# Row-wise cosine similarity: wide operations, a finer last block and an early finish of the first half

## Chip, cores and metric

The kernel runs on one core of one Trainium2 chip. The metric is the time of one execution on the device, in microseconds (us); lower is better. A span is the time from the first to the last instruction in a profile; it is about 1.8 us shorter than the time.

## The reference

For two float32 arrays of 8192 x 8192, one cosine similarity for each row:

```python
x_norm = np.linalg.norm(x, axis=1, keepdims=True)
y_norm = np.linalg.norm(y, axis=1, keepdims=True)
return np.sum(x * y, axis=1) / (x_norm.squeeze() * y_norm.squeeze() + 1e-8)
```

Each row needs three sums: of x·y, of x² and of y². The inputs are 537 MB, and every byte is used once.

## The kernel before

The 8192 rows are 64 blocks of 128 rows, one row for each partition. A block is one tile of x and one of y, 4 MB each. VectorE (DVE) makes the sum of products, ScalarE (ACT) both sums of squares, in two halves of 4096 columns (`CH`). x has three buffers and y two.

```python
def compute_chunk(xt, yt, b, c0, c1, slot):
    w = c1 - c0
    nc.vector.tensor_tensor_reduce(out=prod[:, :w], in0=xt[:, c0:c1], in1=yt[:, c0:c1],
        scale=1.0, scalar=0.0, op0=ALU.mult, op1=ALU.add, accum_out=dps[slot][:, b : b + 1])
    nc.scalar.activation(out=sq[:, :w], in_=xt[:, c0:c1], func=AF.Square, accum_out=sxs[slot][:, b : b + 1])
    nc.scalar.activation(out=sq[:, :w], in_=yt[:, c0:c1], func=AF.Square, accum_out=sys_[slot][:, b : b + 1])

for b in range(nblk):
    # ... cut: the tiles
    if not last:
        if b > 0:
            nc.sync.dma_start(out=xt, in_=x_v[b])
            nc.sync.dma_start(out=yt, in_=y_v[b])
        compute_chunk(xt, yt, b, 0, CH, 0)
        compute_chunk(xt, yt, b, CH, D, 1)
    else:
        cuts = [0, CH, CH + CH // 2, D]
        # ... cut: x and y of each piece are loaded in turn
        for j in range(3):
            compute_chunk(xt, yt, b, cuts[j], cuts[j + 1], j)
```

At the end all 64 columns of sums are added, the root is taken on ACT, DVE makes reciprocal and product, eight 32x32 transposes turn the 128 x 64 result, and one transfer stores it.

## Time and profile before

| what | value | view |
|---|---|---|
| time | 1265.75 us, median of 4 | runs |
| span | 1263.9 us | page |
| load queue | 98.8% of the span of 16 engines | queue table |
| load rate from 60 to 1200 us | 432 GB/s, DMA share 1.00 | stage table |
| DVE, ACT busy | 45%, 75% | page |
| loads end | about 1249 us | stages of 1 us |

The first fence is from the page: busy time of each engine, then the DMA queues with packets, MB and share of time.

```profile
DVE 571.1 (45%) x275; ACT 952.0 (75%) x519; POOL 0.5 (0%) x8
...
q1 hardware_dynamic: 19088, 536.91, 98.8%
q14 instruction: 9, 0.07, 0.0%
```

The second is the stage table of before. Its columns are: stretch in us, its length, busy time of DVE, ACT and POOL with counts of instructions, the granted clock, DMA share, GB/s.

```profile
60.00:1200.00 1140.00, 522.55 (x235) 869.00 (x469) 0.00 (x0) 1.00 1.00 432
...
1245.00:1246.00 1.00, 0.72 (x1) 0.97 (x3) 0.00 (x0) 1.00 0.96 401
1246.00:1247.00 1.00, 1.00 (x1) 1.00 (x1) 0.00 (x0) 1.00 0.26 107
...
1248.00:1249.00 1.00, 0.00 (x0) 1.00 (x2) 0.00 (x0) 1.00 0.14 57
```

The loads run at full rate until 1246 us and trickle out by about 1249. The 15 us after them are the tail. Its timeline follows: start, duration, engine, operation, tile, and in brackets the idle time before it and what ended that.

```profile
1230.45 3.62 ACT L74 ACTIVATE sscr<-yt 128x4096 bf16<-128x4096 f32 x1 [4.50 <-DMA yt<-in_y_dram]
...
1240.32 4.43 DVE L58 CUSTOM_DVE_ANT_0 pscr<-xt,yt 128x4096 bf16<-128x4096 f32 x1 [0.89 <-DMA yt<-in_y_dram]
1241.68 3.62 ACT L68 ACTIVATE sscr<-xt 128x4096 bf16<-128x4096 f32 x1
...
1255.26 1.91 ACT L74 ACTIVATE sscr<-yt 128x2048 bf16<-128x2048 f32 x1
1255.32 0.23 DVE L106 TENSOR_TENSOR sxf<-sxa,sx 128x64 f32<-128x64 f32 x1 [1.86 <-ACT sscr L68]
1255.47 2.29 DVE L58 CUSTOM_DVE_ANT_0 pscr<-xt,yt 128x2048 bf16<-128x2048 f32 x1
...
1257.96 0.22 DVE L112 TENSOR_TENSOR nxny<-sxf,syf 128x64 f32<-128x64 f32 x1
...
1261.07 0.55 SPq L129 DMA_DIRECT2D out_dram<-resT  x1
```

The second-last block's y lands at 1230.4. ACT then works without a pause until 1257, and begins the last block's first square only at 1241.68, though its first y piece, which lands after its x, is there at 1240.3. DVE's last product does not wait for data: it waits behind an add, which waits for ACT.

### The profile page before, as it was taken

To read this page: it belongs to the slowest core of one execution; us is meant where nothing else is said; L and a number is where in the kernel's file an instruction comes from. 1 tells how busy PE (TensorE), PEld (TensorE's weight loads), DVE (VectorE), ACT (ScalarE), POOL (GpSimd) and SP (SyncE) were. 2 spreads that over 40 slices of the span, in tenths; PEclk is the share of its full clock that TensorE was granted. 3 is DMA by queue.
4 is the path that set the end of the run, shared out by engine and by line. 5 is a ranking of instruction groups with operands and counts; after the bars stand their busy time and mean duration, and the time that the engine had idled before them with its cause. 6 is when DMAs were issued, how large, how long until landed. Compare 5 with 4: busy or idle time off the path is not lost.

```text
span 1263.9 us, 1239 instructions
## 1 busy us (share of the span) xinstructions
DVE 571.1 (45%) x275; ACT 952.0 (75%) x519; POOL 0.5 (0%) x8
## 2 busy tenths in 40 slices
DVE  2354353453543534535435345354353453544536
ACT  4787787877877878778777787787777877868777
POOL 0000000000000000000000000000000000000000
DMA  9999999999999999999999999999999999999994
GB/s 398 438 433 431 432 432 432 431 432 433 431 432 432 431 431 431 431 432 431 431 431 431 431 431 431 431 431 433 431 432 431 431 431 431 431 431 431 432 429 189
DMA packets 19097, 536.99 MB, mean 425 GB/s; under 512 B 2128, under 2 KB 2192, under 8 KB 2192
## 3 DMA queue, kind: packets, MB, share of 16 engines
q1 hardware_dynamic: 19088, 536.91, 98.8%
q14 instruction: 9, 0.07, 0.0%
HBM read 536.87 MB, written 0.03 MB: 425 GB/s over the span
## 4 chain that ended last, share of the span: by engine, by line
DMA 70%; ACT 25%; issue 5%; DVE 0%; ACTq 0%; SPq 0%; DVEq 0%
DMA yt<-in_y_dram 70%; ACT sscr L74 15%; ACT sscr L68 9%; DVE pscr L58 0%; DVE resT L125 0%; DVE rsq L117 0%; ACTq L74 0%; SPq L39 0%; ACT den L114 0%; DVE res L119 0%; DVEq L155 0%; DVE nxny L112 0%; DVE syf L106 0%; DVE dpf L106 0%; DVE dp L58 0%
## 5 line engine op out<-in xcount | busy, mean ns | idle before, releaser
L58 DVE CUSTOM_DVE_ANT_0 pscr<-xt,yt 128x4096 bf16<-128x4096 f32 x129 | 566.6, 4392 | 682.3 <-DMA yt<-in_y_dram 680.1
L74 ACT ACTIVATE sscr<-yt 128x4096 bf16<-128x4096 f32 x129 | 463.2, 3590 | 289.8 <-DMA yt<-in_y_dram 287.7
L68 ACT ACTIVATE sscr<-xt 128x4096 bf16<-128x4096 f32 x129 | 463.2, 3590 | 15.0 <-DMA xt<-in_x_dram 11.0
L74 ACT ACTIVATION_READ_ACCUMULATOR sscr<-yt 128x1 f32 x129 | 24.1, 187 | 0.0
L68 ACT ACTIVATION_READ_ACCUMULATOR sscr<-xt 128x1 f32 x129 | 24.1, 187 | 0.0
L58 DVE DVE_READ_ACCUMULATOR2_ANT dp<- 128x1 f32 x129 | 10.6, 82 | 0.0
L105 DVE TENSOR_TENSOR sxa<-sx,sx 128x64 f32<-128x64 f32 x1 | 0.2, 225 | 3.6 <-ACT sscr L68 3.6
L54 ACT ACT_TABLE_LOAD x1 | 1.3, 1283 | 0.7 <-PEq L144 0.7
L125 DVE STREAM_TRANSPOSE resT<-res 32x32 f32<-32x32 f32 x8 | 1.6, 201 | 0.1
L106 DVE TENSOR_TENSOR sxf<-sxa,sx 128x64 f32<-128x64 f32 x1 | 0.2, 225 | 1.9 <-ACT sscr L68 1.9
L105 DVE TENSOR_TENSOR sya<-sy,sy 128x64 f32<-128x64 f32 x1 | 0.2, 227 | 1.7 <-ACT sscr L74 1.7
L114 ACT ACTIVATE den<-nxny 128x64 f32<-128x64 f32 x1 | 0.3, 256 | 0.9 <-DVE nxny L112 0.9
L117 DVE RECIPROCAL rsq<-den 128x64 f32<-128x64 f32 x1 | 0.6, 553 | 0.3 <-ACT den L114 0.3
L119 DVE TENSOR_TENSOR res<-dpf,rsq 128x64 f32<-128x64 f32 x1 | 0.2, 224 | 0.0
L105 DVE TENSOR_TENSOR dpa<-dp,dp 128x64 f32<-128x64 f32 x1 | 0.2, 220 | 0.0
L106 DVE TENSOR_TENSOR syf<-sya,sy 128x64 f32<-128x64 f32 x1 | 0.2, 220 | 0.0
L106 DVE TENSOR_TENSOR dpf<-dpa,dp 128x64 f32<-128x64 f32 x1 | 0.2, 219 | 0.0
L112 DVE TENSOR_TENSOR nxny<-sxf,syf 128x64 f32<-128x64 f32 x1 | 0.2, 218 | 0.0
L54 ACT ACTIVATE rs_warm<-rs_warm 128x1 f32<-128x1 f32 x1 | 0.2, 203 | 0.0
L45 POOL MEMSET dp<- 128x64 f32 x1 | 0.2, 152 | 0.3 <-POOLq L144 0.3
L46 POOL MEMSET sx<- 128x64 f32 x1 | 0.2, 152 | 0.0
L47 POOL MEMSET sy<- 128x64 f32 x1 | 0.2, 152 | 0.0
(5 smaller groups left out, 0.5 us busy)
## 6 DMA issues: line engine op xcount, KB each, us to landing
xt<-in_x_dram SPq DMA_DIRECT2D x63, 4096.0 KB, 36.9
yt<-in_y_dram SPq DMA_DIRECT2D x63, 4096.0 KB, 27.6
xt<-in_x_dram SPq DMA_DIRECT2D x1, 2048.0 KB, 32.1
yt<-in_y_dram SPq DMA_DIRECT2D x1, 2048.0 KB, 17.9
xt<-in_x_dram SPq DMA_DIRECT2D x2, 1024.0 KB, 22.0
yt<-in_y_dram SPq DMA_DIRECT2D x2, 1024.0 KB, 24.0
out_dram<-resT SPq DMA_DIRECT2D x1, 32.0 KB, 1.8
```

The lines of the kernel that those rows point to most:

```text
L45: nc.gpsimd.memset(dps[2], 0.0)
L46: nc.gpsimd.memset(sxs[2], 0.0)
L47: nc.gpsimd.memset(sys_[2], 0.0)
L54: nc.scalar.activation(out=rs_warm, in_=rs_warm, func=AF.Sqrt, bias=0.0)
L58: nc.vector.tensor_tensor_reduce(out=prod[:, :w], in0=xt[:, c0:c1], in1=yt[:, c0:c1], scale=1.0, scalar=0.0, op0=ALU.mult, op1=ALU.add, ac ...
L68: nc.scalar.activation(out=sq[:, :w], in_=xt[:, c0:c1], func=AF.Square, accum_out=sxs[slot][:, b : b + 1],)
L74: nc.scalar.activation(out=sq[:, :w], in_=yt[:, c0:c1], func=AF.Square, accum_out=sys_[slot][:, b : b + 1],)
L105: nc.vector.tensor_tensor(out=a, in0=parts[0], in1=parts[1], op=ALU.add)
L106: nc.vector.tensor_tensor(out=f, in0=a, in1=parts[2], op=ALU.add)
L114: nc.scalar.activation(out=den, in_=nxny, func=AF.Sqrt, bias=0.0)
L117: nc.vector.reciprocal(out=rsq, in_=den)
L125: nc.vector.transpose(out=resT[S * j : S * j + S, S * i : S * i + S], in_=res[S * i : S * i + S, S * j : S * j + S],)
```

## The change

Its intent: one operation of 8192 columns in place of two of 4096 in blocks 0 to 61; the loads of block 62 in halves; the last block in pieces of 4096, 2048, 1024 and 1024, one y square given from ACT to DVE; the first 32 results finished at block 33; the last block's small sums on the idle POOL engine. The core of the diff:

```diff
-                compute_chunk(xt, yt, b, 0, CH, 0)
-                compute_chunk(xt, yt, b, CH, D, 1)
+                ttr(dps[0][:, b : b + 1], xt, yt)
+                square_act(sxs[0][:, b : b + 1], xt)
+                square_act(sys_[0][:, b : b + 1], yt)
+            elif b == nblk - 2:
+                # ... cut: loads of x and y in halves, the same six operations as before,
+                #     then the sums of blocks 32 to 62 into dpf_all and nn_all
             else:
-                cuts = [0, CH, CH + CH // 2, D]
+                # cuts = [0, CH, CH + CH // 2, CH + 3 * CH // 4, D]
+                # ... cut: eight loads: x, y of the first piece, then y, x of each other piece
+                square_act(sxs[0][:, bcol], xc[0])
+                ttr(dps[0][:, bcol], xc[0], yc[0])
+                square_act(sys_[0][:, bcol], yc[0])
+                ttr(sys_[1][:, bcol], yc[1], yc[1])
+                ttr(dps[1][:, bcol], xc[1], yc[1])
+                square_act(sxs[1][:, bcol], xc[1])
+                # ... cut: y square, product, x square for pieces 2 and 3
+                # eight adds on POOL: t_dpa, t_sya, t_sxa, t_syb, t_sxb, t_dpb, t_sy, dpf_all
+                nc.vector.scalar_tensor_tensor(out=nn_all[:, HB - 1 : HB], in0=sxs[3][:, bcol],
+                    scalar=t_sxb, in1=t_sy, op0=ALU.add, op1=ALU.mult)
+            if b == HB + 1:
+                finalize_first_half()   # adds, root, reciprocal, product, four transposes
+        # ... cut: root, reciprocal, product and four transposes for the second half
```

More of the change, by code (lines that the diff above doesn't have):

```diff
@@ L32 @@
     CH = D // 2
+    S = 32
+    HB = nblk // 2
+    cuts = [0, CH, CH + CH // 2, CH + 3 * CH // 4, D]
+    nslot = len(cuts) - 1
     with tc.tile_pool(name="io", bufs=2) as io_pool, tc.tile_pool(
@@ L40 @@
         nc.sync.dma_start(out=yt0, in_=y_v[0])
-        dps = [acc_pool.tile([P, nblk], fp32, name=f"dp{i}") for i in range(3)]
-        sxs = [acc_pool.tile([P, nblk], fp32, name=f"sx{i}") for i in range(3)]
-        sys_ = [acc_pool.tile([P, nblk], fp32, name=f"sy{i}") for i in range(3)]
-        nc.gpsimd.memset(dps[2], 0.0)
-        nc.gpsimd.memset(sxs[2], 0.0)
-        nc.gpsimd.memset(sys_[2], 0.0)
-        prod = scr_pool.tile([P, CH], bf16, name="pscr")
-        sq = scr_pool.tile([P, CH], bf16, name="sscr")
+        dps = [acc_pool.tile([P, nblk], fp32, name=f"dp{i}") for i in range(nslot)]
+        sxs = [acc_pool.tile([P, nblk], fp32, name=f"sx{i}") for i in range(nslot)]
+        sys_ = [acc_pool.tile([P, nblk], fp32, name=f"sy{i}") for i in range(nslot)]
+        for z in (dps[1], sxs[1], sys_[1]):
+            nc.gpsimd.memset(z, 0.0)
+        prod = scr_pool.tile([P, D], bf16, name="pscr")
+        sq = scr_pool.tile([P, D], bf16, name="sscr")
+        resT = acc_pool.tile([nblk, P], fp32, name="resT")
+        dpf_all = acc_pool.tile([P, HB], fp32, name="dpf_all")
+        nn_all = acc_pool.tile([P, HB], fp32, name="nn_all")
+        sxw = acc_pool.tile([P, HB], fp32, name="sxw")
+        syw = acc_pool.tile([P, HB], fp32, name="syw")
+        t_dpa = acc_pool.tile([P, 1], fp32, name="t_dpa")
+        t_dpb = acc_pool.tile([P, 1], fp32, name="t_dpb")
+        t_sxa = acc_pool.tile([P, 1], fp32, name="t_sxa")
+        t_sxb = acc_pool.tile([P, 1], fp32, name="t_sxb")
+        t_sya = acc_pool.tile([P, 1], fp32, name="t_sya")
+        t_syb = acc_pool.tile([P, 1], fp32, name="t_syb")
+        t_sy = acc_pool.tile([P, 1], fp32, name="t_sy")
         rs_warm = acc_pool.tile([P, 1], fp32, name="rs_warm")
@@ L54, with ttr @@
         nc.scalar.activation(out=rs_warm, in_=rs_warm, func=AF.Sqrt, bias=0.0)
-        def compute_chunk(xt, yt, b, c0, c1, slot):
-            w = c1 - c0
+        def ttr(accum, in0, in1):
             nc.vector.tensor_tensor_reduce(
-                out=prod[:, :w],
-                in0=xt[:, c0:c1],
-                in1=yt[:, c0:c1],
+                out=prod[:, : in0.shape[1]],
+                in0=in0,
+                in1=in1,
                 scale=1.0,
@@ L65, in compute_chunk, with square_act, finalize_first_half @@
                 op1=ALU.add,
-                accum_out=dps[slot][:, b : b + 1],
+                accum_out=accum,
             )
+        def square_act(accum, in_):
             nc.scalar.activation(
-                out=sq[:, :w],
-                in_=xt[:, c0:c1],
+                out=sq[:, : in_.shape[1]],
+                in_=in_,
                 func=AF.Square,
-                accum_out=sxs[slot][:, b : b + 1],
+                accum_out=accum,
             )
-            nc.scalar.activation(
-                out=sq[:, :w],
-                in_=yt[:, c0:c1],
-                func=AF.Square,
-                accum_out=sys_[slot][:, b : b + 1],
-            )
+        def finalize_first_half():
+            w = HB
+            c0, c1 = 0, HB
+            sxf = acc_pool.tile([P, w], fp32, name="f0sx")
+            syf = acc_pool.tile([P, w], fp32, name="f0sy")
+            dotf = acc_pool.tile([P, w], fp32, name="f0dp")
+            for parts, f in ((sxs, sxf), (sys_, syf), (dps, dotf)):
+                nc.vector.tensor_tensor(
+                    out=f, in0=parts[0][:, c0:c1], in1=parts[1][:, c0:c1], op=ALU.add
+                )
+            nxny = acc_pool.tile([P, w], fp32, name="f0nn")
+            nc.vector.tensor_tensor(out=nxny, in0=sxf, in1=syf, op=ALU.mult)
+            den = acc_pool.tile([P, w], fp32, name="f0dn")
+            nc.scalar.activation(out=den, in_=nxny, func=AF.Sqrt, bias=0.0)
+            rsq = acc_pool.tile([P, w], fp32, name="f0rs")
+            nc.vector.reciprocal(out=rsq, in_=den)
+            res = acc_pool.tile([P, w], fp32, name="f0re")
+            nc.vector.tensor_tensor(out=res, in0=dotf, in1=rsq, op=ALU.mult)
+            for i in range(P // S):
+                nc.vector.transpose(
+                    out=resT[0:S, S * i : S * i + S],
+                    in_=res[S * i : S * i + S, 0:S],
+                )
         for b in range(nblk):
-            last = b == nblk - 1
             if b == 0:
@@ L87 @@
                 yt = io_pool.tile([P, D], fp32, tag="y", bufs=2)
-            if not last:
+            if b < nblk - 2:
                 if b > 0:
@@ L91 @@
                     nc.sync.dma_start(out=yt, in_=y_v[b])
-                compute_chunk(xt, yt, b, 0, CH, 0)
-                compute_chunk(xt, yt, b, CH, D, 1)
-            else:
-                cuts = [0, CH, CH + CH // 2, D]
-                for j in range(3):
-                    nc.sync.dma_start(out=xt[:, cuts[j] : cuts[j + 1]], in_=x_v[b][:, cuts[j] : cuts[j + 1]])
-                    nc.sync.dma_start(out=yt[:, cuts[j] : cuts[j + 1]], in_=y_v[b][:, cuts[j] : cuts[j + 1]])
-                for j in range(3):
-                    compute_chunk(xt, yt, b, cuts[j], cuts[j + 1], j)
@@ L102, in _sum3 @@
-        def _sum3(parts, nm):
-            a = acc_pool.tile([P, nblk], fp32, name=f"{nm}a")
-            f = acc_pool.tile([P, nblk], fp32, name=f"{nm}f")
-            nc.vector.tensor_tensor(out=a, in0=parts[0], in1=parts[1], op=ALU.add)
-            nc.vector.tensor_tensor(out=f, in0=a, in1=parts[2], op=ALU.add)
-            return f
-        sxf = _sum3(sxs, "sx")
-        syf = _sum3(sys_, "sy")
-        nxny = acc_pool.tile([P, nblk], fp32, name="nxny")
-        nc.vector.tensor_tensor(out=nxny, in0=sxf, in1=syf, op=ALU.mult)
@@ L113 @@
-        den = acc_pool.tile([P, nblk], fp32, name="den")
-        nc.scalar.activation(out=den, in_=nxny, func=AF.Sqrt, bias=0.0)
-        dotf = _sum3(dps, "dp")
-        rsq = acc_pool.tile([P, nblk], fp32, name="rsq")
-        nc.vector.reciprocal(out=rsq, in_=den)
-        res = acc_pool.tile([P, nblk], fp32, name="res")
-        nc.vector.tensor_tensor(out=res, in0=dotf, in1=rsq, op=ALU.mult)
-        resT = acc_pool.tile([nblk, P], fp32, name="resT")
-        S = 32
-        for i in range(P // S):
-            for j in range(nblk // S):
-                nc.vector.transpose(
-                    out=resT[S * j : S * j + S, S * i : S * i + S],
-                    in_=res[S * i : S * i + S, S * j : S * j + S],
-                )
+                ttr(dps[0][:, b : b + 1], xt, yt)
@@ new lines, with add @@
+                square_act(sxs[0][:, b : b + 1], xt)
+                square_act(sys_[0][:, b : b + 1], yt)
+            elif b == nblk - 2:
+                x0, y0 = xt[:, 0:CH], yt[:, 0:CH]
+                x1, y1 = xt[:, CH:D], yt[:, CH:D]
+                nc.sync.dma_start(out=x0, in_=x_v[b][:, 0:CH])
+                nc.sync.dma_start(out=y0, in_=y_v[b][:, 0:CH])
+                nc.sync.dma_start(out=x1, in_=x_v[b][:, CH:D])
+                nc.sync.dma_start(out=y1, in_=y_v[b][:, CH:D])
+                ttr(dps[0][:, b : b + 1], x0, y0)
+                square_act(sxs[0][:, b : b + 1], x0)
+                square_act(sys_[0][:, b : b + 1], y0)
+                ttr(dps[1][:, b : b + 1], x1, y1)
+                square_act(sxs[1][:, b : b + 1], x1)
+                square_act(sys_[1][:, b : b + 1], y1)
+                w2 = nblk - 1 - HB
+                nc.vector.tensor_tensor(
+                    out=dpf_all[:, 0:w2],
+                    in0=dps[0][:, HB : nblk - 1],
+                    in1=dps[1][:, HB : nblk - 1],
+                    op=ALU.add,
+                )
+                nc.vector.tensor_tensor(
+                    out=sxw[:, 0:w2],
+                    in0=sxs[0][:, HB : nblk - 1],
+                    in1=sxs[1][:, HB : nblk - 1],
+                    op=ALU.add,
+                )
+                nc.vector.tensor_tensor(
+                    out=syw[:, 0:w2],
+                    in0=sys_[0][:, HB : nblk - 1],
+                    in1=sys_[1][:, HB : nblk - 1],
+                    op=ALU.add,
+                )
+                nc.vector.tensor_tensor(
+                    out=nn_all[:, 0:w2], in0=sxw[:, 0:w2], in1=syw[:, 0:w2], op=ALU.mult
+                )
+            else:
+                bcol = slice(b, b + 1)
+                xc = [xt[:, cuts[j] : cuts[j + 1]] for j in range(nslot)]
+                yc = [yt[:, cuts[j] : cuts[j + 1]] for j in range(nslot)]
+                xs_hbm = [x_v[b][:, cuts[j] : cuts[j + 1]] for j in range(nslot)]
+                ys_hbm = [y_v[b][:, cuts[j] : cuts[j + 1]] for j in range(nslot)]
+                nc.sync.dma_start(out=xc[0], in_=xs_hbm[0])
+                nc.sync.dma_start(out=yc[0], in_=ys_hbm[0])
+                nc.sync.dma_start(out=yc[1], in_=ys_hbm[1])
+                nc.sync.dma_start(out=xc[1], in_=xs_hbm[1])
+                nc.sync.dma_start(out=yc[2], in_=ys_hbm[2])
+                nc.sync.dma_start(out=xc[2], in_=xs_hbm[2])
+                nc.sync.dma_start(out=yc[3], in_=ys_hbm[3])
+                nc.sync.dma_start(out=xc[3], in_=xs_hbm[3])
+                square_act(sxs[0][:, bcol], xc[0])
[4 more added lines that the diff above has]
+                square_act(sxs[1][:, bcol], xc[1])
+                square_act(sys_[2][:, bcol], yc[2])
+                ttr(dps[2][:, bcol], xc[2], yc[2])
+                square_act(sxs[2][:, bcol], xc[2])
+                square_act(sys_[3][:, bcol], yc[3])
+                ttr(dps[3][:, bcol], xc[3], yc[3])
+                square_act(sxs[3][:, bcol], xc[3])
+                def add(out, a, c):
+                    nc.gpsimd.tensor_tensor(out=out, in0=a, in1=c, op=ALU.add)
+                add(t_dpa, dps[0][:, bcol], dps[1][:, bcol])
+                add(t_sya, sys_[0][:, bcol], sys_[1][:, bcol])
+                add(t_sxa, sxs[0][:, bcol], sxs[1][:, bcol])
+                add(t_syb, t_sya, sys_[2][:, bcol])
+                add(t_sxb, t_sxa, sxs[2][:, bcol])
+                add(t_dpb, t_dpa, dps[2][:, bcol])
+                add(t_sy, t_syb, sys_[3][:, bcol])
+                add(dpf_all[:, HB - 1 : HB], t_dpb, dps[3][:, bcol])
+                nc.vector.scalar_tensor_tensor(
+                    out=nn_all[:, HB - 1 : HB],
+                    in0=sxs[3][:, bcol],
+                    scalar=t_sxb,
+                    in1=t_sy,
+                    op0=ALU.add,
+                    op1=ALU.mult,
+                )
@@ new lines @@
+            if b == HB + 1:
+                finalize_first_half()
+        den2 = acc_pool.tile([P, HB], fp32, name="den2")
+        nc.scalar.activation(out=den2, in_=nn_all, func=AF.Sqrt, bias=0.0)
+        rsq2 = acc_pool.tile([P, HB], fp32, name="rsq2")
+        nc.vector.reciprocal(out=rsq2, in_=den2)
+        res2 = acc_pool.tile([P, HB], fp32, name="res2")
+        nc.vector.tensor_tensor(out=res2, in0=dpf_all, in1=rsq2, op=ALU.mult)
+        for i in range(P // S):
+            nc.vector.transpose(
+                out=resT[HB : HB + S, S * i : S * i + S],
+                in_=res2[S * i : S * i + S, 0:S],
+            )
```

## The prediction

> **What bounds the kernel now.** The loads. The queue table gives their queue 98.8% of the span; the stage table shows 432 GB/s at a DMA share of 1.00 from 60 to 1200 us; DVE is busy 45%, ACT 75%. An x/y pair lands every 19.4 us (timeline), against 8.9 us of DVE and 14.9 us of ACT work. The Trainium skill ("DMA: Bandwidth & Descriptors", "Where 436 GB/s comes from") gives 435 GB/s as the fabric's ceiling; the trace agrees (432), so this part cannot shrink. Outside it lie a start of about 2.5 us and the tail: in windows of 1 us the loads run at full share to 1246 us and trickle out by 1249, while the span ends at 1263.9. A change of the tail can touch 15 us.
>
> **The tail before (timeline).** y of block 62 lands at 1230.4, whole; ACT then has nine dependent squares, through 1257.2, three of block 62 (to 1241.7) while block 63 is landing. DVE's last product starts only at 1255.47, behind an in-order add that waits for ACT, and ends at 1257.7. Adds, root, reciprocal (0.55), product and eight transposes (1.70) end at 1261.04; the output's issue, landing and the end take 2.85.
>
> **What changes.**
> - Steady state: one 8192-wide operation instead of two of 4096. The saved overhead is off the critical path. y's buffer comes free about 8.9 us after landing instead of 11.6, but loads are queued by then: no gain. Finalizing the first half at block 33 blocks DVE for a few us; the loads have slack: no cost.
> - Block 62 in halves: ACT has only y's second half (3.8 us) left at 1230.4, so 7.5 us of backlog goes.
> - Block 63 in pieces, the last 1024 wide. Landings, interpolated from the old waits (y's first half 1240.3, second pieces 1245.2, all by 1249.2); I allow 0.2 us for smaller rows. A 1024-wide square is an estimate of 1.2 us from the old 3.74 and 2.04 us steps. ACT: y's half to 1244.1; x's second piece 1245.4 to 1247.4; four small squares end about 1252.3. DVE: products of 4.55, 2.4 (y squared), 2.4, 1.3, 1.3 from 1240.4 end about 1252.4. Both end 3 us behind the loads.
> - After that: POOL adds, one two-step DVE operation (0.2), root 0.3, reciprocal 0.5, product 0.25, four transposes 0.85 instead of 1.70, then 2.85 unchanged: about 5.0 us.
> - New cost: DVE's last step waits for the seventh of eight POOL adds in order. The skill ("SBUF — State Buffer", "SBUF: two separate sides") says a DVE operation with two SBUF inputs and a POOL operation that reads SBUF exclude each other for a whole instruction. No trace shows it yet. If so, POOL adds slip behind DVE's products and several remain at 1252.4; I allow 1 us (0 to 3).
>
> Span: 1252.4 + 1.0 + 5.0 = 1258.4. Times stand 1.85 us above the span: **1260.2 us**, 0.44% faster; range 1257.8 to 1262.6. Faster by over 2% 0.01, within 2% 0.985, slower 0.005.
>
> **Right if** the steady rate stays 431 to 432 GB/s, loads end within 0.5 us of before, ACT and DVE finish their last pieces near 1252, transposes end at 1255 to 1256. **Wrong if** the final two-step operation waits over 3 us for POOL, or loads thin out in the last 40 us because later issues wait for completions.
>
> **What would spoil it:** a first-use cost of POOL's add at the end; slow small rows; a steady rate that moves by 0.3%, which is 4 us, as much as most of the gain.

## The result

| | before | changed |
|---|---|---|
| time, median | 1265.70 us (13 runs) | 1258.11 us (9 runs, 1257.96 to 1258.84) |
| ratio | | 0.9941 (0.9932 to 0.9951) |
| span of the profiled run | 1263.9 | 1256.6 |

Ratios are the mean time of one kernel's fast runs over that of the other's of the same rounds, so not quite the ratio of the medians.

The page, the stage table and the timeline of the changed kernel, in the same order:

```profile
DVE 563.7 (45%) x159; ACT 914.1 (73%) x274; POOL 5.7 (0%) x16
...
q1 hardware_dynamic: 19664, 536.91, 99.4%
q14 instruction: 7, 0.06, 0.0%
```

```profile
60.00:1200.00 1140.00, 515.16 (x128) 833.62 (x235) 0.00 (x0) 1.00 1.00 432
...
1245.00:1246.00 1.00, 1.00 (x2) 1.00 (x1) 0.00 (x0) 1.00 1.02 410
1246.00:1247.00 1.00, 0.96 (x3) 0.97 (x3) 0.76 (x1) 1.00 0.46 180
...
1248.00:1249.00 1.00, 0.97 (x3) 0.97 (x3) 1.00 (x3) 1.00 0.08 33
```

```profile
1229.46 3.62 ACT L86 ACTIVATE sscr<-yt 128x4096 bf16<-128x4096 f32 x1 [1.18 <-DMA yt<-in_y_dram]
...
1239.29 4.43 DVE L74 CUSTOM_DVE_ANT_0 pscr<-xt,yt 128x4096 bf16<-128x4096 f32 x1 [4.99 <-DMA yt<-in_y_dram]
...
1246.10 2.29 DVE L74 CUSTOM_DVE_ANT_0 pscr<-xt,yt 128x2048 bf16<-128x2048 f32 x1
1246.24 2.20 POOL L192 TENSOR_TENSOR t_sya<-sy,sy 128x1 f32<-128x1 f32 x1 [1245.16 <-ACT sscr L86]
...
1248.43 1.22 DVE L74 CUSTOM_DVE_ANT_0 pscr<-xt,yt 128x1024 bf16<-128x1024 f32 x1
1248.54 1.17 POOL L192 TENSOR_TENSOR t_dpa<-dp,dp 128x1 f32<-128x1 f32 x1
...
1250.77 0.19 ACT L86 ACTIVATION_READ_ACCUMULATOR sscr<-xt 128x1 f32 x1
1250.85 0.08 DVE L74 DVE_READ_ACCUMULATOR2_ANT dp<- 128x1 f32 x1
...
1251.29 0.22 DVE L202 SCALAR_TENSOR_TENSOR nn_all<-sx,t_sxb,t_sy 128x1 f32<-128x1 f32 x1 [0.36 <-POOL t_sy L192]
...
1253.36 0.55 SPq L224 DMA_DIRECT2D out_dram<-resT  x1
```

The load rate has not moved at this precision. ACT now waits for block 62's second half and both engines end the last piece together, at 1250.9. The 7.3 us between the two spans split at three marks that both timelines have:

| stretch | before | changed | gain |
|---|---|---|---|
| start to the last block's first product | 1240.32 | 1239.29 | 1.03 |
| to the multiplication of the two sums of squares | 17.64 | 12.00 | 5.64 |
| to the last transpose's end | 3.08 | 2.05 | 1.03 |
| to the end of the span | 2.86 | 3.26 | -0.40 |

The second and third lines were foreseen. The fourth was not, and neither was the first: this much data came 1 us sooner, although loads and buffers were the same up to block 61.

### The profile page after: what moved, and what is told of

The parts are those of the page before. It is cut to its first block, busy times and chain, and to the rows that moved or that the text cites. A ratio compares the mean times of both kernels' runs of the same rounds, so it can differ in the third digit from the quotient of the medians.

```text
span 1256.6 us, 906 instructions
## 1 busy us (share of the span) xinstructions
DVE 563.7 (45%) x159; ACT 914.1 (73%) x274; POOL 5.7 (0%) x16
## 4 chain that ended last, share of the span: by engine, by line
DMA 77%; DVE 21%; issue 1%; SPq 0%; POOL 0%; DVEq 0%; ACT 0%; ACTq 0%
DMA yt<-in_y_dram 75%; DVE pscr L74 21%; DMA xt<-in_x_dram 2%; POOL t_sya L192 0%; DVEq L74 0%; ACT sscr L86 0%; SPq L126 0%; DVE dp L74 0%; DVE resT L220 0%; SPq L173 0%; SPq L125 0%; SPq L44 0%; SPq L43 0%; DVE rsq L216 0%; SPq L172 0%
## 5 line engine op out<-in xcount | busy, mean ns | idle before, releaser
L74 DVE CUSTOM_DVE_ANT_0 pscr<-xt,yt 128x8192 bf16<-128x8192 f32 (+2 forms) x68 | 556.9, 8190 | 676.0 <-DMA yt<-in_y_dram 675.9
L86 ACT ACTIVATE sscr<-xt 128x8192 bf16<-128x8192 f32 (+2 forms) x68 | 450.7, 6628 | 170.3 <-DMA xt<-in_x_dram 170.1
L86 ACT ACTIVATE sscr<-yt 128x8192 bf16<-128x8192 f32 (+2 forms) x67 | 448.9, 6699 | 164.1 <-DMA yt<-in_y_dram 164.0
L86 ACT ACTIVATION_READ_ACCUMULATOR sscr<-xt 128x1 f32 x68 | 12.7, 187 | 0.0
L86 ACT ACTIVATION_READ_ACCUMULATOR sscr<-yt 128x1 f32 x67 | 12.5, 187 | 0.0
L74 DVE DVE_READ_ACCUMULATOR2_ANT dp<- 128x1 f32 x68 | 5.6, 82 | 0.0
## 6 DMA issues: line engine op xcount, KB each, us to landing
yt<-in_y_dram SPq DMA_DIRECT2D x62, 4096.0 KB, 29.9
```

Source lines behind the costliest of these rows:

```text
L74: nc.vector.tensor_tensor_reduce(out=prod[:, : in0.shape[1]], in0=in0, in1=in1, scale=1.0, scalar=0.0, op0=ALU.mult, op1=ALU.add, accum_ou ...
L86: nc.scalar.activation(out=sq[:, : in_.shape[1]], in_=in_, func=AF.Square, accum_out=accum,)
```

## The experiments

### Where does the earlier landing come from?

Theory A: loads alone set the pace, so wide operations give nothing there. The rivals were that y is released earlier, and that fewer instructions help. Four runs on the same chip came first: e1 and e2 here, e3 and e4 in the next part.

**e1_wide61**: the kernel before with wide operations in blocks 0 to 61.

```diff
-                compute_chunk(xt, yt, b, 0, CH, 0)
-                compute_chunk(xt, yt, b, CH, D, 1)
+                if b < nblk - 2:
+                    compute_chunk(xt, yt, b, 0, D, 0)
+                else:
+                    compute_chunk(xt, yt, b, 0, CH, 0)
+                    compute_chunk(xt, yt, b, CH, D, 1)
```

(and the second set of sums is zeroed at the start, the scratch is 8192 wide)

> The kernel before, with one 8192-wide operation in place of two of 4096 in blocks 0 to 61 only; its tail is untouched. Theory A (the loads alone set the pace, nothing of the steady state is gained): time within 0.2 us of before, second-last y landing at 1230.4 us of the span. Theory B (the 1.0 us by which the changed kernel's loads land earlier comes from the wide operations, through earlier release of y or fewer instructions): 0.8 to 1.1 us faster, y of block 62 near 1229.4.

Measured: 1264.25 us against 1265.59, so 1.34 faster, a little more than theory B gave; ACT begins on block 62's y at 1229.25. Theory A falls. The instruction queue (the DMA queue that brings the engines their instructions) had 6 packets in this run where before had 9. The first line is from this run's page, the second from its timeline:

```profile
q14 instruction: 6, 0.05, 0.0%
...
1229.25 3.62 ACT L77 ACTIVATE sscr<-yt 128x4096 bf16<-128x4096 f32 x1 [6.00 <-DMA yt<-in_y_dram]
```

**e2_xxyy**: the kernel before with ACT's order x, x, y, y in blocks 0 to 62.

```diff
-                compute_chunk(xt, yt, b, 0, CH, 0)
-                compute_chunk(xt, yt, b, CH, D, 1)
+                # both products as before, then:
+                for src, parts in ((xt, sxs), (yt, sys_)):
+                    for half in range(2):
+                        c0 = half * CH
+                        nc.scalar.activation(out=sq[:, :CH], in_=src[:, c0 : c0 + CH],
+                            func=AF.Square, accum_out=parts[half][:, b : b + 1])
```

> The kernel before, with 4096-wide operations kept, but ACT squares both halves of x before both halves of y, in blocks 0 to 62; loads untouched. y is then released as early as in the changed kernel, and ACT has only 7.5 us left of block 62 when its y lands, so that it waits for block 63 as in the changed kernel. Theory A: 3.9 us faster (ACT's last square ends near 1253.3 in place of 1257.1), landings as before. Theory B by earlier release: 4.8 us faster, landings 1 us earlier. Theory B by fewer instructions: 3.9.

Measured: 1261.88, so 3.71 faster. ACT begins on block 62's y at 1230.33, as before (1230.45), though y's buffer is released as early as in the changed kernel (29.7 us from a y load's issue to its landing against 27.6 before, 29.9 in the changed kernel). Earlier release is therefore not the cause. From this run's timeline:

```profile
1230.33 3.62 ACT L107 ACTIVATE sscr<-yt 128x4096 bf16<-128x4096 f32 x1 [2.26 <-DMA yt<-in_y_dram]
```

The traces show what is. The next fence is DVE's timeline of the kernel before: the first product of each of four blocks, each of which starts just after its y lands. After it, the DMA view of the same kernel from 883 to 884 us.

```profile
860.06 4.43 DVE L58 CUSTOM_DVE_ANT_0 pscr<-xt,yt 128x4096 bf16<-128x4096 f32 x1 [10.53 <-DMA yt<-in_y_dram]
...
879.50 4.42 DVE L58 CUSTOM_DVE_ANT_0 pscr<-xt,yt 128x4096 bf16<-128x4096 f32 x1 [10.53 <-DMA yt<-in_y_dram]
...
899.61 4.43 DVE L58 CUSTOM_DVE_ANT_0 pscr<-xt,yt 128x4096 bf16<-128x4096 f32 x1 [11.22 <-DMA yt<-in_y_dram]
...
919.03 4.43 DVE L58 CUSTOM_DVE_ANT_0 pscr<-xt,yt 128x4096 bf16<-128x4096 f32 x1 [10.52 <-DMA yt<-in_y_dram]
```

```profile
q1 hardware_dynamic: 8, 0.26, 61.0%
q14 instruction: 1, 0.01, 2.0%
```

These products start 19.44, 20.11 and 19.42 us apart. Nearly every pair in every trace takes 19.43; the long one is the pair in whose time a packet of the instruction queue ran. This packet's 2.0% of 16 engines' microsecond is about 0.32 us of one engine. By the landing times that the traces keep, six of the eight packets of before up to block 61 fall into long pairs, of 19.58 to 20.12, and two into pairs of 19.43 and 19.44. In all traces, with wide operations or without, every pair in which no packet ran takes 19.41 to 19.45.

**n1_fetch** gives more of them: 1024 memsets of a dummy column on POOL, which nothing waits for, in the kernel before.

```diff
+        dummy = acc_pool.tile([P, 1], fp32, name="dummy")
+        for _ in range(1024):
+            nc.gpsimd.memset(dummy, 0.0)
```

> The kernel before with 1024 memsets of a dummy column on POOL, which nothing waits for. In all traces so far an x/y pair lands every 19.43 us, but the pair that meets a packet of the instruction queue takes 0.2 to 0.7 us longer; the kernel before has nine such packets, the changed one seven, the one with wide blocks six. Theory F (each fetch of instructions delays the loads, and fewer instructions is why the changed kernel's loads land 1 us earlier): the dummies bring 5 to 9 more packets, the affected pairs take 0.2 to 0.7 us longer, and the kernel is 1.5 to 5 us slower, all of it visible in the landing of the last y. Rival (the long pairs come of something else, and the wide operations free the loads in another way): within 0.3 us of before, no more long pairs than before.

Measured: 1267.30 against 1265.55, 1.75 slower. Its instruction queue had 17 packets, eight more. The queue's line of its page, and DVE's timeline, first products of the first four blocks:

```profile
q14 instruction: 17, 0.14, 0.0%
...
23.07 4.42 DVE L62 CUSTOM_DVE_ANT_0 pscr<-xt,yt 128x4096 bf16<-128x4096 f32 x1 [23.07 <-DMA yt<-in_y_dram]
...
43.16 4.42 DVE L62 CUSTOM_DVE_ANT_0 pscr<-xt,yt 128x4096 bf16<-128x4096 f32 x1 [11.20 <-DMA yt<-in_y_dram]
...
63.27 4.42 DVE L62 CUSTOM_DVE_ANT_0 pscr<-xt,yt 128x4096 bf16<-128x4096 f32 x1 [11.20 <-DMA yt<-in_y_dram]
...
83.33 4.42 DVE L62 CUSTOM_DVE_ANT_0 pscr<-xt,yt 128x4096 bf16<-128x4096 f32 x1 [11.16 <-DMA yt<-in_y_dram]
```

They are 20.09, 20.11 and 20.06 apart; in the kernel before the same three are 19.46, 19.42 and 19.43. The first seven pairs are long here, as long as the dummies are being fetched. The memsets themselves run on POOL to 161.4 us, over the same seven pairs, so this run alone does not part them from their fetches; but the long pairs of before are as long (up to 20.12), with POOL idle. The rival of "something else" falls. One thing was not foreseen: this run's later packets, most of which made long pairs in before, cost nothing. By landings all later pairs take 19.41 to 19.44. (By first products one of them is 19.82 and the next 19.02, because DVE began that block 0.56 us after its y had landed in place of 0.16.) So a packet does not always cost time, and why some do not is open.

The table sums it up. "Extra" is the time from the first product of block 0 to that of block 61, less 61 times 19.43; packets are those of the instruction queue in the time up to then.

| kernel | packets | extra us |
|---|---|---|
| before | 8 | 2.85 |
| e2_xxyy, e3_half62, e4_early | 8 each | 3.00, 2.91, 2.86 |
| changed; its control c1_after | 6 each | 1.99; 1.57 |
| the six other runs with the changed steady state | 6 each | 1.47 to 2.04 |
| e1_wide61 | 5 | 1.79 |
| n1_fetch | 16 | 4.35 |

So of the changed kernel's 1.03 us, 0.86 is less extra time. Another 0.29 is that the changed kernel's first product starts earlier (22.73 in place of 23.02); this scatters as much between runs whose start is the same (22.75 in e2_xxyy). And 0.12 was lost again in the last two blocks.

The Trainium skill ("Runtime: NRT & Kernel Launch", "Instruction fetch mechanics") says that each engine's sequencer fetches its instructions by DMA in blocks, and that this is "mostly hidden". It was hidden from POOL in n1_fetch, whose 1024 memsets start every 0.16 us, without a gap. Where loads are the bound, these traces show it in the loads.

### What was the tail's backlog worth?

**e3_half62**: only block 62's loads are cut in halves.

```diff
-                if b > 0:
+                if b == nblk - 2:
+                    for c0 in (0, CH):
+                        nc.sync.dma_start(out=xt[:, c0 : c0 + CH], in_=x_v[b][:, c0 : c0 + CH])
+                        nc.sync.dma_start(out=yt[:, c0 : c0 + CH], in_=y_v[b][:, c0 : c0 + CH])
+                elif b > 0:
```

> The kernel before, with the loads of block 62 alone cut in halves (four lines); operations and their order untouched. If the backlog of ACT at block 62 is what made the tail late: 3.9 us faster, ACT's last square ends near 1253.3, DVE's last product near 1253.8. If DVE's in-order chain or the landings set it: less than 1.5 us.

Measured: 1261.09, so 4.50 faster. These four lines of the edit give most of the change's gain. ACT's last square starts at 1250.71 in its timeline (before: 1255.26), and DVE's last product at 1250.93 (before: 1255.47):

```profile
1250.71 1.91 ACT L74 ACTIVATE sscr<-yt 128x2048 bf16<-128x2048 f32 x1
...
1250.93 2.29 DVE L58 CUSTOM_DVE_ANT_0 pscr<-xt,yt 128x2048 bf16<-128x2048 f32 x1
```

The gain is 0.6 more than expected because ACT does not wait at all from 1210.94 on, where an idle gap had been reckoned with. e2_xxyy, which reaches the same by order alone, has that gap (2.26 us of waiting for y of block 62) and gains 3.71. So it is the backlog that counted, and either a load in halves or another order of ACT's work removes it.

**e4_early**: the kernel before with the first half's results finished at block 33.

```diff
+            if b == HB + 1:
+                finalize(0, 2)   # adds, root, reciprocal, product, four transposes of blocks 0 to 31
 ...
-        # the same for all 64 columns, eight transposes
+        finalize(1, 3)           # blocks 32 to 63
```

> The kernel before, with the first 32 blocks' results finished at block 33, so that the end has four transposes in place of eight and 32-wide operations in place of 64: 1.1 us faster (four transposes at 0.21, reciprocal 0.2, five small operations at 0.03). If finishing at block 33 held up a load, the loads' share would dip near 660 us and some of this would be lost.

Measured: 1264.49, so 1.10 faster, as expected. Its landings are those of before: finishing in the middle held up nothing.

**n4_y1act**: the changed kernel with the second y piece's square back on ACT.

```diff
-                ttr(sys_[1][:, bcol], yc[1], yc[1])
+                square_act(sys_[1][:, bcol], yc[1])
```

> The changed kernel with the square of y's second piece back on ACT in place of DVE. If ACT and DVE are balanced at the end and ACT has 1.3 us of idle to give: ACT's last square ends near 1251.8 in place of 1251.0, 0.7 us slower than the changed kernel. If ACT were the only bound, the full 2.0 us; if DVE were, faster.

Measured: 1258.79, 0.68 slower than the changed kernel's 1258.11 (in other rounds: before was 1265.55 in these and 1265.70 in those). ACT's last square is read out at 1251.48 in place of 1250.77. The square on DVE is worth a third of its 2.0 us, since ACT had been idle for 1.3 us there.

### What do the POOL adds cost?

In the changed kernel `t_sya` lasts 2.20 us and `t_dpa` 1.17, for one column. Each ends just where the product beside it ends; adds that fall between products last 0.19.

**p1_lock** tests this with probes on POOL in the steady state (one look, state unknown; only durations are used).

```diff
+                if b in (10, 11):   # ready when y's squares are done
+                    nc.gpsimd.tensor_tensor(out=pr_y, in0=sys_[0][:, b : b + 1], in1=sys_[0][:, b : b + 1], op=ALU.add)
+                if b in (20, 21):   # ready when x's squares are done
+                    nc.gpsimd.tensor_tensor(out=pr_x, in0=sxs[0][:, b : b + 1], in1=sxs[0][:, b : b + 1], op=ALU.add)
+                if b in (40, 41):
+                    nc.scalar.activation(out=pr_m, in_=sys_[0][:, b : b + 1], func=AF.Square)
+                    nc.gpsimd.memset(pr_m, 0.0)
+                if b in (50, 51):
+                    nc.gpsimd.tensor_scalar(out=pr_w, in0=xt[:, :2048], scalar1=sxs[0][:, b : b + 1], scalar2=None, op0=ALU.add)
```

> The changed kernel with four POOL probes in blocks of the steady state, where DVE has slack, so that the time does not matter. Theory L (a product of DVE with two SBUF inputs and a POOL operation that reads SBUF exclude each other): an add of one column that becomes ready when ACT ends y's squares, 1.6 us before the 8.69 us product ends, lasts about 1.6 us; the same add ready while DVE is idle lasts 0.19 us; a memset, which reads nothing, ready at the first moment lasts 0.10 us; and a 2048-wide read on POOL that starts about 2.6 us before y lands holds up the product if it lasts longer than that. Rival (POOL's add is slow by itself the first time or now and then): the adds of blocks 10 and 11 last as long as those of 20 and 21, or only the first is long.

The timeline of this run, the product that surrounds a probe and the probe:

```profile
217.24 8.69 DVE L78 CUSTOM_DVE_ANT_0 pscr<-xt,yt 128x8192 bf16<-128x8192 f32 x1 [10.81 <-DMA yt<-in_y_dram]
...
224.36 1.62 POOL L135 TENSOR_TENSOR pr_y<-sy 128x1 f32<-128x1 f32 x1 [223.29 <-ACT sscr L90]
...
408.92 0.19 POOL L139 TENSOR_TENSOR pr_x<-sx 128x1 f32<-128x1 f32 x1 [163.51 <-ACT sscr L90]
...
808.11 0.10 POOL L144 MEMSET pr_m<- 128x1 f32 x1 [378.86 <-ACT pr_m L143]
...
992.48 5.44 POOL L146 TENSOR_SCALAR pr_w<-xt,sx 128x2048 bf16<-128x2048 f32 x1 [164.78 <-ACT sscr L90]
...
995.05 9.68 DVE L78 CUSTOM_DVE_ANT_0 pscr<-xt,yt 128x8192 bf16<-128x8192 f32 x1 [10.73 <-DMA yt<-in_y_dram]
```

The product ends at 217.24 + 8.69 = 225.93, the add inside it at 225.98; alone the add takes 0.19, and the memset inside a product (not shown: 800.78 to 809.47) 0.10. The pairs of probes agree (1.62 and 1.55; 0.19 twice; 0.10 twice). This is what the skill states ("SBUF — State Buffer", "Who interferes with whom"): a DVE instruction with two SBUF inputs contends with a POOL instruction that reads SBUF, not with one that only writes it. In the other direction the product is slowed, 9.68 in place of 8.69, but by 1.0 us, and not by the 2.87 for which the two overlap in the profile.

**n2_dpdve**: three of the eight adds become two operations of DVE.

```diff
-                add(t_dpa, dps[0][:, bcol], dps[1][:, bcol])
-                add(t_dpb, t_dpa, dps[2][:, bcol])
-                add(dpf_all[:, HB - 1 : HB], t_dpb, dps[3][:, bcol])
+        nc.vector.scalar_tensor_tensor(out=t_dpb, in0=dps[0][:, bcol], scalar=dps[1][:, bcol],
+            in1=dps[2][:, bcol], op0=ALU.add, op1=ALU.add)
+        nc.vector.tensor_tensor(out=dpf_all[:, HB - 1 : HB], in0=t_dpb, in1=dps[3][:, bcol], op=ALU.add)
```

> The changed kernel with the three adds of the dot products taken from POOL and made two operations of DVE; five adds stay on POOL. If the order of POOL's eight adds is what delays the final two-step operation by 0.36 us: 0.1 to 0.3 us faster than the changed kernel's 1258.1. If POOL's adds are blocked by DVE's products whatever they are: the same within 0.1 us, with t_sy still ending just after the last product. POOL's t_sya and t_sxb should again last exactly until a product ends.

Measured: 1257.96. `t_sy` still lasts to the last product's end (1.20 us), but nothing is left behind it, and the two-step operation follows the product without a wait. `t_sya` lasted until a product's end again (2.20); `t_sxb` did not, it fell between two products (0.19). From the first product to it are 11.85 us, against 12.00 in the changed kernel. Both expectations hold in part; the gain, 0.15 us, is within the scatter of the runs.

**n3_dveadds**: all eight adds on DVE.

```diff
-                    nc.gpsimd.tensor_tensor(out=out, in0=a, in1=c, op=ALU.add)
+                    nc.vector.tensor_tensor(out=out, in0=a, in1=c, op=ALU.add)
```

> The changed kernel with all eight small adds on DVE and none on POOL. DVE's chain grows by six or seven operations of 0.12 to 0.19 us before the final two-step operation: 0.5 to 1.0 us slower than the changed kernel if POOL's delay is only the 0.36 us that the trace shows. If the exclusion of POOL and DVE also slows DVE's own products or costs more than that: the same or faster.

Measured: 1258.32, 0.2 slower, less than expected: the seven adds before the two-step operation cost DVE's chain some 0.43 us (12.06 from the first product's start to the last one's end, in place of 11.63), as they follow each other every 0.07 to 0.12 us. From the first product to the two-step operation are 11.98 us. POOL's delay of 0.36 us and DVE's own adds are worth the same within the scatter; moving the adds to the idle engine gained nothing that these runs can show.

### Is there a better version?

**c1_after** is the control: the changed kernel unedited, on the chip of the next two.

> The changed kernel again, unedited, as the control on the same chip for the next two: 7.5 us faster than before.

Measured: 1258.20 against 1265.60.

**b1_cuts**: the last block in pieces of 2048, 2048, 2048, 1024 and 1024, all squares on ACT, all adds on DVE.

```diff
-    cuts = [0, CH, CH + CH // 2, CH + 3 * CH // 4, D]
+    cuts = [0, CH // 2, CH, CH + CH // 2, CH + 3 * CH // 4, D]
 ...
+                for j in range(nslot):
+                    square_act(sys_[j][:, bcol], yc[j])
+                    square_act(sxs[j][:, bcol], xc[j])
+                    ttr(dps[j][:, bcol], xc[j], yc[j])
+                # ... cut: seven adds on DVE
```

> The changed kernel with the last block cut in pieces of 2048, 2048, 2048, 1024, 1024, all squares on ACT, only products on DVE, no POOL adds. In the changed kernel DVE idles 5 us before the last block's first product and then runs without a wait for 11.6 us, ending 2 us behind the loads. If that late start is what is left: DVE and ACT end about 1.2 us after the last load, near 1250.0, and it is 0.8 to 1.2 us faster than the changed kernel. If more pieces cost the loads more than that: no gain.

Measured: 1258.08, no gain. DVE starts early now (1234.55), but from the third x piece on (1244.45) ACT runs without a wait to 1251.2: five squares, 2.0 and four times 1.2 us, against the 4 us in which the rest of the data lands. And DVE's last product, at 1250.14, again stands behind an add that waits 0.81 us for ACT. The estimate had looked at DVE's late start and had forgotten that ACT is the fuller engine without the square that DVE took.

**b2_column**: b1_cuts, with 63 blocks' results stored early and the last block's stored as a column, with no transposes.

```diff
+        nc.sync.dma_start(out=out_v[0 : nblk - 1], in_=resT[0 : nblk - 1])
+        # ... cut: root, reciprocal and product of one column
+        nc.sync.dma_start(out=out_c[nblk - 1], in_=rescol)   # 128 partitions x 4 bytes
-        nc.sync.dma_start(out=out_v, in_=resT)
```

> The kernel of b1_cuts, with 63 blocks' results finished, transposed and stored before the last block is done, and the last block's 128 results stored as a column, without transposes. The end saves four transposes (0.85) and 0.25 of the narrower reciprocal; a store of 128 separate words may cost up to 0.5 more than one of 64 rows: 0.6 to 1.1 us faster than b1_cuts. If the store of 63 rows delays the last loads, less.

Measured: 1261.65, 3.6 slower than b1_cuts. The last store is issued at 1252.07, 1.22 sooner than in b1_cuts (1253.29), but its landing is late. From the DMA issues of b2_column (size, median us from issue to landing):

```profile
out_dram<-rescol SPq DMA_DIRECT2D x1, 0.5 KB, 7.2
```

and of the changed kernel:

```profile
out_dram<-resT SPq DMA_DIRECT2D x1, 32.0 KB, 1.9
```

A store of 64 rows of 512 bytes lands in 1.9 us, one of 128 separate words in 7.2. The transfers themselves ran from 1252.93 to 1253.13; what is late is the landing, at 1259.32. The store of the 63 rows had run by 1248.9, so it is not what held it up. The expectation's allowance of 0.5 us for the words had no measurement behind it. The skill ("DMA: Bandwidth & Descriptors", "Specifications") gives 512 bytes as the least for full rate and a read-modify-write below it; it gives no such delay. No version tried beats the changed kernel by more than the scatter.

## Why the prediction was right, and where it was off

The time, 1258.11, lies in the stated range, 2.1 below the stated value and only 0.3 above the range's lower end. Of the four marks under "Right if", only the rate held as written: the last load landed 0.86 us sooner than before (1249.17 against 1250.03), the last pieces ended 1 us before 1252, and the transposes ended at 1253.34 and not at 1255 to 1256. The terms:

- *Loads bind the steady state and the rate does not change.* Right: 432 GB/s in both stage tables, near the ceiling of 435 that the skill gives ("DMA: Bandwidth & Descriptors", "Where 436 GB/s comes from").
- *"The saved overhead is off the critical path ... no gain."* This step failed: the last block's first product starts 1.03 us sooner. The engines' time was off the path, as said; the fetches of their instructions were not. n1_fetch shows that packets lengthen pairs, e1_wide61 that wide operations alone bring 1.34 us with fewer packets, e2_xxyy that earlier release of y brings nothing. Pairs without a packet take 19.41 to 19.45 with wide operations and without, so nothing else of their form is seen to help. The earlier landing is half of the miss; of its 1.03 us the fetches account for about 0.9, the rest is scatter of the start.
- *Earlier release of y gives nothing.* Right (e2_xxyy).
- *Finishing the first half costs no load.* Right (e4_early).
- *ACT's backlog of block 62 goes.* Right in mechanism; e3_half62 shows that it alone is worth 4.5 us.
- *ACT and DVE end together at 1252.3 and 1252.4.* They ended together, at 1250.96 and 1250.93. Of the 1.5 us, 1.03 are the earlier landing; the rest is DVE's chain, 11.64 us from its first product in place of 12.0.
- *POOL waits for DVE's products: 1 us.* Right in mechanism (p1_lock), mis-sized: DVE waited 0.36, since only three of the eight adds were left when the last product ended: two had run in gaps between products and three had been stretched beside them.
- *Final chain 5.0.* It took 5.31: the stretch after the last transpose is 3.26 in place of 2.85. The output lands 1.88 us after the last transpose in both; the extra comes after that, among SyncE's closing instructions. A packet of the instruction queue falls in the last half microsecond of the changed kernel (at 1256.4), and none does in before, but it is not needed: n4_y1act has the same 3.26, and its last packet starts only after the span's end. The cause stays open.

The sum of the errors, which in part cancel: -1.03 and -0.4 to the pieces' end, -0.64 for POOL, +0.3 at the end; -1.8 for the span, 1256.6 in place of 1258.4. The remaining 0.3 is that the profiled run was 0.28 above the median.

## What to carry to other kernels

Where loads are the bound to the end, what counts is the work that an engine still has to do when the last data arrives: look at the queue of the fuller engine one block before the end, not only at the last block, and cut the loads or order the work so that it enters the last block with nothing left over. Count instructions, too: on this kernel, which runs at full DMA rate, two or three fetches fewer were worth about 1 us in the landings. Moving small operations to an idle engine gains nothing when they are then held up by the work of the engine they were to relieve, as the adds were here, and a few bytes stored in separate words can cost more (7.2 us to land) than the transposes that avoid them (0.85).

## What the Trainium skill lacked or had wrong

- "Runtime: NRT & Kernel Launch", "Instruction fetch mechanics": blocks of 16 KiB with 256 instructions, "mostly hidden". Here a packet is about 8 KB (17 packets, 0.14 MB), and 1024 more instructions brought 8 packets, so 128 each; in the kernel before one packet lengthened a pair of loads by up to 0.69 us (19.43 to 20.12).
- "SBUF — State Buffer", "SBUF: two separate sides": the loser blocks fully for the whole instruction. A POOL add under a product did (to the product's end, up to 2.20 us). A product that started under a POOL read of 2048 columns lost 1.0 us of the 2.87 of overlap that the profile shows; POOL's spans are rough.
- "DMA: Bandwidth & Descriptors" has no figure for a store of single words: 128 words of 4 bytes took 7.2 us to land, 64 rows of 512 bytes 1.9.
